# A list scheduler gets a shared SBUF interface and re-measured instruction times

## The chip, the cores and the metric

The kernel runs on one core of a Trainium2 chip. A core has engines that run side by side and wait for each other by semaphores: TensorE (PE in the profile; its weight loads are the row PEld), VectorE (DVE), ScalarE (ACT), GpSimd (POOL) and SyncE (SP), which here issues all DMAs. The metric is the device time in microseconds of one execution. Before the change it is 1359.93 us, the median of three runs (1359.56 to 1360.98).

## The reference, cut to what matters

Two layers of a diffusion block over 256 latent tokens `x` and 256 context tokens `ctx`, 1024 features each, all float32:

```python
for l in range(DEPTH):                                   # 2 layers
    mod_x = silu(c) @ w_ada[l] + b_ada[l]                # shift, scale, gate; the same for ctx
    hx = rms_norm(x, norm_w[l]) * (1 + scale_x) + shift_x
    px = split(hx @ w_in[l], ...)                        # one wide input projection
    y_a = window_sink_attention(...)                     # 8 heads, 2 key heads
    y_b = neighborhood_attention(...)                    # 8 heads, a learned 2-D bias
    y_c = dense_block_attention(...)                     # 8 heads, 2 key heads
    y_d = differential_attention(...)                    # 4 heads of two softmaxes
    branches = [y * silu(gate) for each mixer]
    x = x + gate_x * (sum_n sigmoid(g_n) * (branch_n @ w_br[l, n])) @ w_out[l]
    # the context tokens go the same way, but for the last layer's output
```

Queries and keys of every head are RMS-normed; those of A, C and D get a rotary embedding.

## The kernel before

The program multiplies in float32 by splitting each operand in two float32r parts. A weight chunk of 128 x 1024 comes by DMA as `raw`; its high part `wh` is a rounding copy (ACT or DVE), its low part `wl` is the subtraction `raw - wh` (DVE or POOL). Each matmul of the definition is then three: high by high, high by low, low by high (`mm3`). The chunks are handled in halves of up to 512 columns, and there are 520 of these low-part subtractions. Activations are split in the same way (`hT`, `yT`, `K`, `Q`, `t4k`, `V`). The adaLN products are dot products on DVE (`raw`, `t2k` with `scb`), some on POOL and PE.

All work is written as a sequence of calls, which a `Recorder` collects instead of issuing (class `Recorder`, its engines all record in one line, L270, so in the profile every instruction stands under L270). `alt` makes one operation of each call: the engines that could do it (`ways`), a time for each (`cost`), the operations that it depends on. `copy`, `tt` and `scale` are calls that leave a choice: ACT or DVE for copies (`AV`), DVE or POOL for two-input elementwise work between SBUF tiles (`VG`).

`schedule` is then a list scheduler with a clock of its own. For each engine it looks through the first 60 operations that are available, in order of priority, and takes the first one that could start at once, or else the one that could start first (`ready`: its producers' ends plus a latency from `LAT`, its tiles' slots, its PSUM banks). Where an operation has two ways, it goes to the engine where its end plus `BIAS` (0.55 us for DVE, 0.35 for ACT, 0 for POOL) is earlier. The engine whose candidate can start first gets the next place. `deadlines` works out from the finished schedule how late each operation might start without making TensorE late, and these become the priorities of the next of six tries (`search`); the try whose model ends first is issued, engine by engine, in its order. So the two tables that the change touches, `cost` and the conditions in `ready`, set which engine does what and in which order; the instructions themselves, their shapes and the amount of TensorE's work are the same for every schedule.

On the chip each engine then runs its list in order and waits for semaphores; the planned times are not enforced. GpSimd's `pow` operations (tile `st` with `expo`) are the inverse roots of the norms.

Names in the rows: `ppj`, `psc`, `ptr` are PSUM tiles of projections, scores and transposes; `qk` holds queries or keys before their transposition, `st` columns of statistics, `P` the softmax numerators, `t4k` the transposed numerators, `merged` the gated sum of branches, `bias` mixer B's table.

Of the kernel before, what the change touches and what calls it, by code (L numbers as in the profile page):

```python
# [14 lines left out]
F32R = mybir.dt.float32r  # L15
BF16 = mybir.dt.bfloat16
AF = mybir.ActivationFunctionType
ALU = mybir.AluOpType
# [18 lines left out]
# the grid's tokens go column by column, so that 128 of them are half of the grid. Mixer B's keys: one half, the  # L37
# context, the other half; a half's windows reach 8 columns into the other one
# [5 lines left out]
# token-major groups: blocks of 128 columns (mixer, q/k/v/g, index);  # L44
# "S?" is a mixer's gate path and "G??" a merge gate, both feature-major.
# [34 lines left out]
# the adaLN units computed after a group: the next layer's scale and shift, this layer's gate  # L80
# [9 lines left out]
# ---- instruction order: the program is recorded first, then each engine's order is chosen by list  # L90
# scheduling against a model of the engines, and issued in that order ----
ADA = "DPDDGDDGPGGDDGDD"                       # layer 0, shift and scale: units on VectorE (D), GpSimd (G), TensorE (P)
# [8 lines left out]
GATE = 4096 / 1200.0                         # TensorE runs at half its clock after such a time with little work  # L101
# from the end of an instruction to the start of one that needs it; for TensorE with some margin, so that what it
# has in hand covers a late operand
# [10 lines left out]
def _extent(ap):  # L114
    """(partition range, range of elements within a partition's row) that an access pattern touches"""
# [19 lines left out]
def _run(ap):  # L135
    """elements of the contiguous pieces"""
    return ap.ap[-1][1] if ap.ap[-1][0] == 1 else 1
# [13 lines left out]
# PSUM banks are shared by the three uses, each of which is sure of some  # L151
# [22 lines left out]
class Recorder:  # L174
    def __init__(self, nc, pools, plan=None):
# [3 lines left out]
        if plan is not None:                     # tiles are allocated in the order in which the plan uses them  # L179
            self.made = {}  # L180
            for k, slot in plan.slots:
                self.made[k] = self.make(plan.spec[k], slot)
# [3 lines left out]
        self.acc = {}                            # tile name -> [(op, write, extent)]  # L186
        self.tag = {}                            # tile name -> (tag, bufs)
# [1568 lines left out]
```

## Time and profile before

| | before |
|---|---|
| median of three runs | 1359.93 us |
| profiled execution, first to last instruction (span) | 1355.9 us |
| PE busy | 1266.3 us, 7286 matmuls |
| PEld busy | 1086.5 us |
| DVE busy | 1094.4 us, 2108 instructions |
| ACT busy | 741.8 us, 1738 instructions |
| POOL busy | 696.1 us, 694 instructions |
| mean granted TensorE clock | 0.981 of full speed |
| DMA engines busy | 37.3% |

The time of the profiled execution itself is not listed beside its span; against the median of the runs the span leaves 1359.93 - 1355.9 = 4.0 us for what lies ahead of the first and behind the last instruction. Busy time counts an instruction from its start to its end, so an instruction that is held up after its start counts as busy for as long as it is held. A PE that is busy is not PE at its peak, since matmuls overlap; idle time of an engine counts against the run only where another engine that sets the end waits for it. Stages can be told apart by time: up to about 200 us the adaLN products and the first projection, then the rest of layer 0, from about 800 us layer 1.

### The profile page before, as it was taken

What the parts mean: (1) busy time and instruction counts of PE and PEld (TensorE: products, weight loads), DVE (VectorE), ACT (ScalarE), POOL (GpSimd) and SP (SyncE); (2) the same over time, 40 slices, a digit from 0 to 9 for tenths busy, and PEclk for the clock granted to TensorE, in tenths of its full rate; (3) what the DMA queues carried; (4) which work ended last, traced back from release to release, by engine and by line L of the source; (5) the groups of instructions that cost most, each with busy time, mean ns of one, the idle gap of its engine ahead of it and who ended that gap; (6) DMA issues with size and microseconds to landing.
All of it is one profiled execution on the core that took longest, in us unless ns stands there. A gap on an engine that the chain in (4) does not pass through costs nothing. (4 is left out here: it accounts for less than half of the span.)

```text
span 1355.9 us, 21375 instructions
## 1 busy us (share of the span) xinstructions
PE 1266.3 (93%) x7286; PEld 1086.5 (80%) x7286; DVE 1094.4 (81%) x2108; ACT 741.8 (55%) x1738; POOL 696.1 (51%) x694
## 2 busy tenths in 40 slices
PE   7688999999999999999999999899999899899998
PEld 5466778789877989778777887888889899788897
DVE  7999974974998688995788568798995878886877
ACT  6466843463765346633456345577664556554563
POOL 4784224424554655534364236665754756475643
PEclk8899999999999999999999999999999999999999
DMA  6531133313322432243322266231436534343454
GB/s 244 179 123 42 47 105 98 124 58 114 90 87 94 147 114 72 88 153 100 105 63 78 85 208 203 81 125 51 138 114 176 166 121 140 100 127 105 143 168 172
DMA packets 64576, 160.90 MB, mean 119 GB/s; under 512 B 13482, under 2 KB 24914, under 8 KB 64468
## 3 DMA queue, kind: packets, MB, share of 16 engines
q1 hardware_dynamic: 64468, 159.55, 37.3%
q8 instruction: 57, 0.93, 0.3%
q14 instruction: 51, 0.42, 0.1%
HBM read 157.42 MB, written 5.88 MB: 120 GB/s over the span
## 5 line engine op out<-in xcount | busy, mean ns | idle before, releaser
L270 POOL TENSOR_TENSOR wl<-raw,wh 128x512 fp32r<-128x512 f32 (+2 forms) x233 | 307.6, 1324 | 341.0 <-PE ppj L270 179.6
L270 PE MATMUL ppj<-wh,hT 128*128 128x512 f32 (+2 forms) x1424 | 388.2, 351 | 18.5 <-DVE hT L270 14.2
L270 ACT ACTIVATE wh<-raw 128x512 fp32r<-128x512 f32 (+2 forms) x394 | 233.3, 600 | 250.7 <-PE ppj L270 187.9
L270 PE MATMUL ppj<-hT,wh 128*128 128x512 f32 (+1 forms) x1408 | 368.5, 345 | 0.0
L270 PEld LDWEIGHTS ppj<-wh,hT 128*128 128x128 f32 x1424 | 253.5, 192 | 45.1 <-DVE hT L270 16.8
L270 PEld LDWEIGHTS ppj<-hT,wh 128*128 128x128 f32 x1408 | 244.0, 191 | 27.4 <-ACT t2k L270 0.2
L270 DVE TENSOR_TENSOR wl<-raw,wh 128x512 fp32r<-128x512 f32 (+2 forms) x247 | 199.5, 817 | 77.9 <-PE ppj L270 63.3
L270 PE MATMUL ppj<-wl,hT 128*128 128x512 f32 (+2 forms) x712 | 248.3, 349 | 1.2 <-DVE wl L270 0.7
L270 PE MATMUL ppj<-hT,wl 128*128 128x512 f32 (+1 forms) x704 | 242.9, 345 | 1.8 <-DVE wl L270 1.8
L270 PEld LDWEIGHTS ppj<-wl,hT 128*128 128x128 f32 x712 | 136.8, 192 | 14.8 <-POOL wl L270 1.6
L270 ACT ACTIVATE P<-psc,st 128x512 f32<-128x512 f32 (+2 forms) x192 | 114.8, 601 | 60.8 <-DVE st L270 53.3
L270 PEld LDWEIGHTS ppj<-hT,wl 128*128 128x128 f32 x704 | 134.4, 191 | 16.0 <-DVE wl L270 2.5
L270 PE MATMUL ppj<-yT,wh 128*128 128x512 f32 (+1 forms) x512 | 131.7, 341 | 0.4 <-DVE yT L270 0.4
L270 PE MATMUL psc<-K,Q 128*128 128x512 f32 (+2 forms) x384 | 99.1, 367 | 13.8 <-DVE Q L270 8.4
L270 PE MATMUL ptr<-ident,P 128*128 128x128 f32 x560 | 88.1, 277 | 17.4 <-DVE P L270 12.5
L270 DVE TENSOR_REDUCE st<-psc 128x1 f32<-128x512 f32 (+2 forms) x160 | 102.3, 660 | 1.0
L270 POOL TENSOR_TENSOR st<-st,expo 128x8 f32<-128x8 f32 (+3 forms) x68 | 97.5, 1437 | 2.5
L270 PEld LDWEIGHTS ppj<-yT,wh 128*128 128x128 f32 x512 | 87.5, 189 | 10.6 <-DVE yT L270 0.8
L270 PEld LDWEIGHTS ptr<-ident,P 128*128 128x128 f32 x560 | 64.9, 141 | 37.6 <-DVE P L270 10.3
L270 PEld LDWEIGHTS psc<-K,Q 128*128 128x128 f32 x384 | 63.6, 192 | 33.2 <-DVE Q L270 12.0
L270 PE MATMUL ptr<-t4k,V 128*128 128x256 f32 x480 | 78.4, 289 | 11.1 <-DVE t4k L270 9.0
L270 PE MATMUL ppj<-yT,wl 128*128 128x512 f32 (+1 forms) x256 | 86.8, 339 | 1.0 <-DVE wl L270 1.0
(176 smaller groups left out, 2139.2 us busy)
## 6 DMA issues: line engine op xcount, KB each, us to landing
raw<-in_w_G SPq DMA_DIRECT2D x64, 512.0 KB
raw<-in_w_ada SPq DMA_DIRECT2D x43, 512.0 KB
raw<-in_w_br SPq DMA_DIRECT2D x32, 512.0 KB
raw<-in_w_in_D SPq DMA_DIRECT2D x32, 512.0 KB
raw<-in_w_S SPq DMA_DIRECT2D x24, 512.0 KB
raw<-in_w_in_B SPq DMA_DIRECT2D x32, 384.0 KB
raw<-in_w_out SPq DMA_DIRECT2D x24, 512.0 KB
raw<-in_w_in_A SPq DMA_DIRECT2D x8, 512.0 KB
```

Of the source, the lines that this page charges most:

```text
L270: getattr(getattr(self.nc, eng), fn)(*args, **kw)
```

## The change

Two things change in the planner, nothing in what is computed. `alt` keeps for each way of an operation whether it uses an SBUF interface that DVE and POOL are taken to share (`shares`), and `schedule` lets such an operation start only after the last such operation of the other engine has ended. And `cost` gets other times: float32r matmuls 0.4475 ns a column (before, 1/2400 us, and at least the stationary operand's columns over 1200), ACT 0.08 us more on 64 partitions, DVE 0.06 us more on 64 partitions with PSUM, POOL elementwise 0.1 + 2.35 ns an element (before, 0.15 + 2.1 ns), POOL's `pow` 0.33 + 0.175 us a column, its short `tensor_scalar` 0.23 us. The rest of the diff takes comments out, by which line L270 becomes L271.

```diff
@@ alt
-        op.ways, op.costs = ways, {}
+        op.ways, op.costs, op.port = ways, {}, {}
...
             op.costs[eng] = self.cost(eng, fn, outs, ins, args, kw)
+            op.port[eng] = self.shares(eng, fn, outs, ins, kw)
@@ cost
+        half = outs[0].shape[0] == 64
         if eng == "tensor":
             n = _count(outs[0])
-            f = 1.0 if ins[0].dtype in (F32R, BF16) else (2.0 if fn == "transpose" else 4.0)
-            return max(f * n / 2400.0, _count(ins[0]) / 1200.0) + 0.003
+            if ins[0].dtype in (F32R, BF16):
+                return 0.0028 + n * 0.4475e-3
+            return 0.109 if fn == "transpose" else n * 1.8e-3
         if eng == "scalar":
...
-            return (0.051 if psum else 0.094) + n / 1200.0 + 0.093 * aps
+            return (0.051 if psum else 0.094) + n / 1200.0 + 0.093 * aps + 0.08 * half
...
-            return (62 + n) / 960.0 + (0.06 * aps if fn in ("scalar_tensor_tensor", "tensor_scalar") else 0.0)
+            return (62 + n) / 960.0 + (0.06 * aps if fn in ("scalar_tensor_tensor", "tensor_scalar") else 0.0) + (
+                0.06 * (half and psum))
         if eng == "gpsimd":
             if kw.get("op") == ALU.pow:
-                return 0.3 + 0.165 * n
-            return 0.15 + n * (0.0021 if fn != "tensor_scalar" else 0.0034)
+                return 0.33 + 0.175 * n
+            if fn == "memset":
+                return 0.14
+            if fn == "tensor_scalar":
+                return 0.23 if n < 50 else 0.15 + 0.0103 * n
+            return 0.1 + n * 0.00235
+
+    @staticmethod
+    def shares(eng, fn, outs, ins, kw):
+        if fn == "dma_start" or eng not in ("vector", "gpsimd"):
+            return False
+        if eng == "gpsimd":
+            return kw.get("op") != ALU.pow and _count(outs[0]) >= 16
+        if any(z.space == PSUM for z in outs + ins):
+            return False
+        return fn in ("tensor_copy", "tensor_scalar", "memset") or sum(_count(z) > 1 for z in ins) > 1
@@ schedule
+        port = dict.fromkeys(ENGS, 0.0)
+
         def ready(o, e, s):
             r = max(o.at[e], s)
+            if o.port[e]:
+                r = max(r, port["gpsimd" if e == "vector" else "vector"])
...
             o.fin = t_free[e] = t + c
+            if o.port[e]:
+                port[e] = o.fin
```

What the planner makes of it: of the 520 low-part subtractions 95 go from POOL to DVE and 52 from DVE to POOL; 65 rounding copies `wh` go from DVE to ACT and 27 from ACT to DVE; 62 products that norm or scale `qk` go from DVE to POOL and 20 the other way. Counted by shape, `wl` of 512 columns stands 168 times on POOL before and 106 times after (216 and 278 on DVE); POOL's `wl` of 384 and 256 columns go from 41 to 54 and from 24 to 30; `wh` of 512 columns goes from 74 to 40 on DVE and from 310 to 344 on ACT; POOL's `qk` products with `st` or `gain` go from 35 to 52 (256 columns with `st`), 18 to 28 (128 with `st`) and 5 to 17 (128 with `gain`).

The first place is in layer 1, where mixer D's keys and queries are normed (`qk<-qk,st`) while weight chunks are split. VectorE's list there before:

```order
L270 TENSOR_TENSOR t2k<-of,gT 128x256
L270 TENSOR_TENSOR qk<-qk,st 128x256
L270 TENSOR_TENSOR wl<-raw,wh 128x512
L270 TENSOR_TENSOR yT<-t2k,yT 128x256
L270 TENSOR_TENSOR qk<-qk,st 128x128 x2
L270 CAST wh<-raw 128x512
L270 TENSOR_TENSOR wl<-raw,wh 128x512
```

VectorE's list at the same place now:

```order
L271 TENSOR_REDUCE st<-t2k 128x2
L271 TENSOR_TENSOR wl<-raw,wh 128x512 x4
L271 TENSOR_TENSOR of<-ptr,t2k 64x256
L271 TENSOR_TENSOR V_3083<-ppj,V_3083 128x2x64
L271 TENSOR_TENSOR wl<-raw,wh 128x512 x2
L271 TENSOR_TENSOR Q_3136<-ptr,Q_3136 64x256 x2
L271 CAST yT<-t2k 128x256
```

GpSimd's list at that place before:

```order
L270 TENSOR_TENSOR st<-st,expo 128x8
L270 TENSOR_SCALAR st<-st 128x4
L270 TENSOR_TENSOR qk<-qk,st 128x256
L270 TENSOR_TENSOR st<-st,expo 128x4
L270 TENSOR_TENSOR wl<-raw,wh 128x512
L270 TENSOR_TENSOR bias<-bias,maskB 128x320 x2
L270 TENSOR_TENSOR wl<-raw,wh 128x512 x2
```

GpSimd's list at that place now:

```order
L271 TENSOR_SCALAR st<-st 128x4
L271 TENSOR_TENSOR st<-st,expo 128x4
L271 TENSOR_TENSOR qk<-qk,st 128x128
L271 TENSOR_TENSOR wl<-raw,wh 128x512
L271 TENSOR_TENSOR qk<-qk,gain 128x128
L271 TENSOR_TENSOR bias<-bias,maskB 128x320
L271 TENSOR_TENSOR qk<-qk,st 128x128
L271 TENSOR_TENSOR bias<-bias,maskB 128x320
L271 TENSOR_TENSOR t2k<-of,gT 128x256
L271 TENSOR_TENSOR yT<-t2k,yT 128x256
```

The products `qk<-qk,st` and the split `yT` went from VectorE to GpSimd, and the low parts of 512 columns from GpSimd to VectorE, which now has six of them there.

The second place is in layer 0, where keys and queries of one unit come out of the transposition (64x512, from PSUM) while the first branch is merged. VectorE's list before:

```order
L270 TENSOR_TENSOR wl<-raw,wh 128x512
L270 SCALAR_TENSOR_TENSOR merged<-th,ppj 128x512
L270 CAST K_680<-ptr 64x512
L270 TENSOR_TENSOR K_680<-ptr,K_680 64x512
L270 TENSOR_TENSOR Q_681<-ptr,Q_681 64x512 x2
L270 SCALAR_TENSOR_TENSOR merged<-th,ppj 128x512
L270 TENSOR_TENSOR K_680<-ptr,K_680 64x512 x3
```

VectorE's list there now:

```order
L271 SCALAR_TENSOR_TENSOR merged<-th,ppj 128x512
L271 TENSOR_TENSOR wl<-raw,wh 128x512
L271 TENSOR_TENSOR Q_680<-ptr,Q_680 64x512 x2
L271 SCALAR_TENSOR_TENSOR merged<-th,ppj 128x512
L271 CAST wh<-raw 128x512
L271 TENSOR_TENSOR K_681<-ptr,K_681 64x512 x4
```

The two operations on `Q` now stand ahead of all four on `K`, and the rounding copy of `K` is no longer among them (the buffer numbers differ between the two programs; the tiles are the same).

## Rows read from the trace of the kernel before

**Rows 1.** The page's span, and busy time by engine (share, instructions).

```profile
span 1355.9 us, 21375 instructions
...
PE 1266.3 (93%) x7286; PEld 1086.5 (80%) x7286; DVE 1094.4 (81%) x2108; ACT 741.8 (55%) x1738; POOL 696.1 (51%) x694
```

**Rows 2.** Busy time by stretch: PE, PEld, DVE, ACT, POOL; granted clock, DMA share, GB/s.

```profile
0.00:200.00 200.00, 167.88 (x841) 130.27 (x842) 180.61 (x351) 119.97 (x279) 100.51 (x89) 0.93 0.38 123
200.00:800.00 600.00, 580.89 (x2958) 484.33 (x2957) 460.87 (x848) 303.62 (x709) 269.38 (x259) 1.00 0.32 99
800.00:1300.00 500.00, 465.89 (x3125) 423.74 (x3124) 414.01 (x849) 295.41 (x706) 309.10 (x330) 0.98 0.43 134
1300.00:1356.00 56.00, 51.67 (x368) 48.13 (x366) 38.91 (x61) 22.82 (x45) 17.12 (x17) 1.00 0.51 169
```

**Rows 3.** Waits of PE after 200 us: waiter, releaser, us in total, times, longest.

```profile
PE ptr L270 <- DVE P L270: 10.0, 15, 1.8
PE psc L270 <- DVE Q L270: 8.4, 8, 3.3
PE ptr L270 <- DVE t4k L270: 7.8, 12, 1.3
...
PE ppj L270 <- DVE yT L270: 0.4, 1, 0.4
```

**Rows 4.** The chain that ended last, its longest piece: start, us, engine, matmuls.

```profile
757.41 54.11 PE ppj L270 x234
```

**Rows 5.** Timeline from 1164 to 1168 us, lines of POOL, DVE and PE.

```profile
1164.41 1.18 POOL L270 TENSOR_TENSOR st<-st,expo 128x4 f32<-128x4 f32 x1
...
1164.65 0.41 DVE L270 TENSOR_TENSOR qk<-qk,st 128x256 f32<-128x256 f32 x1
...
1165.56 1.56 POOL L270 TENSOR_TENSOR wl<-raw,wh 128x512 fp32r<-128x512 f32 x1
...
1165.92 2.22 DVE L270 TENSOR_TENSOR qk<-qk,st 128x128 f32<-128x128 f32 x2
...
1167.08 0.91 POOL L270 TENSOR_TENSOR bias<-bias,maskB 128x320 f32<-128x320 f32 x1
...
1167.32 0.33 PE L270 MATMUL ptr<-ident,qk 128*128 128x128 f32 x1 [2.25 <-DVE qk L270]
```

**Rows 6.** DVE's groups by shape: count, busy us, mean ns, idle before.

```profile
L270 DVE TENSOR_TENSOR wl<-raw,wh 128x512 fp32r<-128x512 f32 x216 | 176.5, 827 | 70.7 <-PE ppj L270 60.4 <-ACT wh L270 4.9 <-POOL st L270 1.4
...
L270 DVE TENSOR_TENSOR t4k<-ptr,t4k 128x512 fp32r<-128x512 f32 x112 | 76.1, 680 | 6.3 <-ACT t4k L270 5.6
...
L270 DVE CAST wh<-raw 128x512 fp32r<-128x512 f32 x74 | 54.7, 740 | 7.9 <-PE ppj L270 5.5 <-issue 2.4
...
L270 DVE TENSOR_TENSOR st<-st,nsink 128x1 f32<-128x1 f32 x32 | 9.9, 311 | 0.1
```

**Rows 7.** Timeline, one rounding copy on DVE that nothing holds up.

```profile
348.70 0.43 DVE L270 CAST wh<-raw 128x512 fp32r<-128x512 f32 x1
```

**Rows 8.** Groups by shape on DVE, POOL and ACT, as in group 6.

```profile
L270 POOL TENSOR_TENSOR wl<-raw,wh 128x512 fp32r<-128x512 f32 x168 | 242.8, 1448 | 275.0 <-PE ppj L270 128.5 <-ACT wh L270 44.8 <-issue 19.6
...
L270 ACT ACTIVATE wh<-raw 128x512 fp32r<-128x512 f32 x310 | 193.5, 631 | 184.2 <-PE ppj L270 133.1 <-issue 11.9 <-DVE t2k L270 9.6
...
L270 POOL TENSOR_TENSOR st<-st,expo 128x8 f32<-128x8 f32 x36 | 65.4, 1817 | 1.2
...
L270 DVE RECIPROCAL st<-st 128x1 f32<-128x1 f32 x96 | 14.4, 152 | 0.3
```

**Rows 9.** Timeline from 253.8 to 257 us, lines of DVE and PE.

```profile
253.84 0.67 DVE L270 CAST K<-ptr 64x512 fp32r<-64x512 f32 x1
254.54 0.68 DVE L270 TENSOR_TENSOR K<-ptr,K 64x512 fp32r<-64x512 f32 x1
255.26 1.41 DVE L270 TENSOR_TENSOR Q<-ptr,Q 64x512 fp32r<-64x512 f32 x2
...
256.00 0.85 PE L270 MATMUL psc<-K,Q 128*128 128x512 f32 x3 [3.33 <-DVE Q L270]
```

## The prediction

> **What bounds the kernel now.** I read the busy times first. PE is busy for 1266.3 of 1355.9 us, DVE for 1094.4, and no other engine passes 55% [rows 1]. PE's work is the same for every schedule, so a schedule can only give back what PE loses: 1355.9 - 1266.3 = 89.6 us of idle time, and what it runs at the lower clock. By stretch [rows 2], PE is idle for 200 - 167.9 = 32.1 us up to 200 us, 19.1 us up to 800, 34.1 us up to 1300 and 4.3 us at the end (the last evictions and the store). Behind 800 us the mean clock is 0.98: over 500 us that is 10 us at full speed lost to stretches at 1.2 instead of 2.4 GHz.
>
> Who is waited for? Of PE's waits after 200 us [rows 3] twelve lines name DVE; from 10.0 us for `P` down to 0.4 us for `yT` they sum to 43.8 us. The eight others name POOL and ACT and are short. So DVE is what PE waits for, though DVE has idle time of its own, 1355.9 - 1094.4 = 261.5 us. The question is why it is late.
>
> The timeline at one of the longest waits shows it [rows 5]. At 1165.56 POOL starts a low part of 512 columns. DVE comes to two products `qk<-qk,st` of 128 columns at 1165.92 and needs 2.22 us for the two, although one of 256 columns took 0.41 us a moment before. The first cannot end before POOL's subtraction does, at 1167.12, and the second not before POOL's next instruction, which began at 1167.08 and ends at 1167.99. PE stands for 2.25 us. DVE and POOL hold each other out for whole instructions.
>
> How much of this is in DVE's busy time is read by comparing equal sizes [rows 6]: `t4k`, with 512 columns and one operand in PSUM, takes 680 ns on average; `wl`, with 512 columns and both in SBUF, 827. That is 216 x 0.147 = 31.8 us of being held. A rounding copy `wh` alone takes 0.43 us [rows 7], on average 0.740 [rows 6]: 74 x 0.31 = 22.9 us. These two groups hold 55 us of waiting; they are not all.
>
> **The change part by part.** *Load.* By the counts of the section on the change POOL loses 62 low parts of 512 columns at 1.448 us [rows 8], 89.8 us, and gets 13 of 384 and 6 of 256 columns (by columns, estimates of 1.09 and 0.72 us: 14.1 and 4.3 us), and 39 `qk` products, which I put at 0.72 us for 17 of 256 columns and 0.36 for 22 of 128, by the same price a column: 20.2 us. Net, POOL has 51 us less of 696. DVE gets 62 x 0.68 = 42.2 us by `t4k` [rows 6] and gives 34 x 0.43 = 14.6 us of copies to ACT [rows 7], 19 smaller low parts (13 x 0.51 + 6 x 0.34 = 8.7 us) and the 39 products (17 x 0.41 + 22 x 0.28, estimates from the 0.41 us of [rows 5], about 13 us): net +6 us without waits. ACT gets 34 x 0.631 = 21.5 us [rows 8] on 742, which its idle time hides: it is busy for 55%. None of these loads lies on the path by itself; what counts is when DVE is late.
>
> *Order with the interface known.* It has no row in the trace of before, so I bound it. From above: every wait for DVE after 200 us goes, and with it the lower clock: 43.8 + 10 = 54 us. From below: since only the order is issued and not the planned times, the two engines may meet as by chance as before, just more rarely; POOL holds the interface for 51 of 696 us less, 7%, and 7% of 43.8 is 3 us. Nothing excludes a loss either; it is a rival below. Between these ends I take two places. At the first one [rows 5] the products now stand on POOL itself, and their 2.25 us of being held there can't arise in that form. At the second [rows 9], PE waited 3.33 us for `Q` while DVE did the copy and one subtraction of `K` first, 0.67 and 0.68 us; now `Q` stands ahead of `K`, worth about 1.35 us. Together 3.6 of 5.6 us, 64%. These are two of the longest waits, DVE now has six low parts in a row at the first place, and an order that ends one wait makes others, so I take half rather than 64%: 22 us of waits and 5 us of clock.
>
> *The first 200 us.* Half of PE's idle time there is the start, which the order hardly changes: weights come in one fixed order, and the adaLN products fill DVE (180.6 of 200 us busy [rows 2]). I count nothing.
>
> *The times.* The longest unbroken run of matmuls, all of 512 columns, gives 54.11 / 234 = 0.231 us each [rows 4]. The old table says 0.216, the new one 0.232. So in the old plan PE ran 7% too fast against its helpers, and DVE, by the waits, too fast as well. The correction has no price of its own in the sum; the slower rival is built on it.
>
> **Where a rule of the notes and the rows meet.** The root operations `pow` do not hold DVE up in the trace: while POOL was in one of 1.18 us, DVE's product took its usual 0.41 us [rows 5]. The new rule leaves `pow` out, in keeping with that. The Trainium skill, "SBUF — State Buffer", section "Who interferes with whom", says that a VectorE instruction with two SBUF inputs contends with any GpSimd instruction that reads SBUF, for the whole instruction. By the page the change would leave some 65 us of holding unplanned in the largest `pow` group alone (36 x 1.817 us, [rows 8]) and I would expect less than half; by the row it leaves none, and I go by the row.
>
> On one-column operations the trace says the opposite of the new rule: a two-input `st<-st,nsink` of one column takes 311 ns on average [rows 6], a reciprocal of one column 152 [rows 8]. The new function counts only inputs of more than one element, so these stay unplanned: 32 x 0.16 = 5 us of waiting that the change cannot take away, part of the half that I leave. The same page names two SBUF inputs, whatever their size, and the trace agrees.
>
> **The rivals.** *Chance meetings stay.* The chip does not keep the plan's times: weights and semaphores come earlier or later, and DVE and POOL meet about as often as their load says. For it speaks that nothing enforces the times; against it that both lists changed so that work which would collide now often stands on one engine. The gain is 3 us, up to a third of what I forecast: 1348 to 1357 us; at the low end this is no change at all.
>
> *Nearly all waits go.* DVE is idle for 261 us and has much work on PSUM operands, which is not held up (`t4k`, [rows 6]), so an order with few meetings is possible. Then 54 us: 1306 us. Against it: POOL's and DVE's users together are still a large share of the time, and the one-column ones aren't planned.
>
> *Lost margin, slower.* With matmuls planned 0.015 us too short each, a block of 24 of 512 columns gave every helper 0.36 us that the plan didn't count on. That margin goes with the new table, and helpers are placed as late as their own times allow. Place: the matmuls that need scores' and transposes' operands (`psc`, `ptr`), where PE's waits are now. There are 70 waits in the 20 lines of [rows 3]; each longer by 0.36 us costs 25 us, and less the 3 us of the lower load the run takes 1382 us. It decides where the plan's helper times are short by more than the plan's own latencies leave. Against it: the interface wait, which was the largest error in the helpers' times, is now planned.
>
> **How the numbers follow.** The profiled execution spans 1355.9 us; the median of the runs is 4.0 us more, and I carry these 4 us along. Forecast: 1359.9 - 22 - 5 = 1333 us; with the ends of the half (a third to three quarters of 54 us) 1319 to 1345. Chances: forecast 0.46; chance meetings with a gain that shows 0.18; nearly all waits gone 0.12; no change 0.08; slower 0.16. A measurement of this kernel can tell about 0.2% from no change, here 2.7 us. Faster by more than that is 0.46 + 0.18 + 0.12 = 0.76, within it 0.08, slower 0.16. The range for 8 in 10 leaves out the lower half of the large gain (0.06) and most of the slower case (0.13): 1308 to 1367 us.
>
> **What would show it.** If I am right, DVE's busy time falls by 40 us or more although its work grows by 6: `wl` of 512 columns comes from 827 ns down towards 690, `wh` on DVE from 740 towards 430, one-column `st<-st,nsink` stays near 300. The lines of PE's waits that name DVE sum to about 22 us after 200 us, and the clock behind 800 us is 0.99. If meetings stay by chance, these means stay within 10% of before. If the margin is lost, `wl` gets faster and PE's waits at `ptr` and `psc` grow all the same, in number above all. I am wrong in the large if PE's idle time up to 200 us moves by more than 10 us, or if ACT, with 21 us more, becomes what PE waits for.

## The result and the profile after

The changed kernel takes 1321.45 us, the median of four runs (1319.68 to 1325.38), beside 1360.28 us for the kernel before on the same chip (four runs, 1359.56 to 1360.98). The ratio is 0.9721, with a 95% interval of 0.9705 to 0.9738: 38.8 us less. Forecast were 27 us less (1333) in a range of 1308 to 1367. Sign and mechanism held, the size was 1.4 times the forecast, and behind that size stand three errors that partly cancel; the experiments take them apart.

The page of the kernel after, its span and busy times by engine (share, instructions), to be read beside [rows 1]:

```profile
span 1317.9 us, 21363 instructions
...
PE 1243.6 (94%) x7286; PEld 1083.4 (82%) x7286; DVE 1003.8 (76%) x2074; ACT 757.1 (57%) x1761; POOL 626.9 (48%) x705
```

The span is 38.0 us shorter. PE's idle time fell from 89.6 to 74.3 us, by 15.3. The other 22.7 us came out of PE's *busy* time, 1266.3 to 1243.6, with the same 7286 matmuls. DVE's busy time fell by 90.6 us, although by the counts it has some 6 us more to do: it was being held, and is held less now.

Busy time by stretch in the kernel after (PE, PEld, DVE, ACT, POOL; then granted clock, DMA share, GB/s), against [rows 2]:

```profile
0.00:200.00 200.00, 156.36 (x816) 124.72 (x817) 165.80 (x342) 119.59 (x281) 94.92 (x90) 0.91 0.37 121
200.00:800.00 600.00, 593.43 (x3044) 500.69 (x3043) 441.56 (x879) 312.96 (x721) 230.72 (x247) 1.00 0.35 107
800.00:1270.00 470.00, 450.48 (x3135) 418.45 (x3134) 364.35 (x804) 303.43 (x720) 287.87 (x355) 0.99 0.45 137
1270.00:1318.00 48.00, 43.31 (x296) 39.55 (x294) 32.09 (x50) 21.09 (x40) 13.35 (x13) 1.00 0.51 173
```

Behind 200 us PE is idle for 6.6 + 19.5 + 4.7 = 30.8 us where it was 57.5. In the first 200 us it is idle for 43.6 us where it was 32.1: that part got worse by 11.5 us. The mean clock behind 800 us is 0.99 where it was 0.98; in the first 200 us it is 0.91 where it was 0.93. Over the whole span it is 0.981 in both.

The waits of PE after 200 us in the kernel after (waiter, releaser, us in total, times, longest), against [rows 3]:

```profile
PE ptr L271 <- DVE P L271: 5.1, 5, 3.3
PE ptr L271 <- DVE Q L271: 4.4, 2, 3.5
PE ptr L271 <- DVE t4k L271: 2.8, 4, 0.9
PE ptr L271 <- ACT P L271: 2.6, 2, 1.8
PE psc L271 <- ACT P L271: 2.0, 3, 1.2
PE psc L271 <- DVE Q L271: 1.9, 2, 1.4
```

Together the lines that name DVE hold 17.9 us in 20 waits, where they held 43.8 us in 59.

DVE's and POOL's groups by shape in the kernel after (count, busy us, mean ns of one, idle before), against [rows 6] and [rows 8]:

```profile
L271 DVE TENSOR_TENSOR wl<-raw,wh 128x512 fp32r<-128x512 f32 x278 | 204.5, 748 | 85.8 <-PE ppj L271 58.8 <-ACT wh L271 14.0 <-issue 8.0
...
L271 DVE TENSOR_TENSOR t4k<-ptr,t4k 128x512 fp32r<-128x512 f32 x112 | 76.5, 683 | 5.7 <-ACT t4k L271 4.2
...
L271 DVE CAST wh<-raw 128x512 fp32r<-128x512 f32 x40 | 19.6, 494 | 4.7 <-PE ppj L271 2.5 <-POOL wl L271 2.0
...
L271 DVE TENSOR_TENSOR st<-st,nsink 128x1 f32<-128x1 f32 x32 | 7.1, 225 | 0.1
...
L271 POOL TENSOR_TENSOR wl<-raw,wh 128x512 fp32r<-128x512 f32 x106 | 140.4, 1329 | 227.2 <-PE ppj L271 110.9 <-ACT wh L271 61.4 <-issue 13.7
```

The same instruction on the same data got shorter: a low part on DVE 827 to 748 ns, one on POOL 1448 to 1329, a rounding copy on DVE 740 to 494. `t4k`, which has an operand in PSUM, stayed (680, now 683). So the two engines stand in each other's way less, in both directions.

At the second place, DVE and PE from 254.7 us in the kernel after (start, us, engine; in brackets what ended the idle time before it), against [rows 9]:

```profile
254.75 0.68 DVE L271 TENSOR_TENSOR wl<-raw,wh 128x512 fp32r<-128x512 f32 x1
...
256.24 1.41 DVE L271 TENSOR_TENSOR Q<-ptr,Q 64x512 fp32r<-64x512 f32 x2 [0.81 <-ACT Q L271]
...
257.00 0.39 PE L271 MATMUL ppj<-hT,wl 128*128 128x512 f32 x1
257.23 0.63 PE L271 MATMUL ppj<-hT,wh 128*128 128x512 f32 x2
257.68 0.69 DVE L271 SCALAR_TENSOR_TENSOR merged<-th,ppj 128x512 f32<-128x512 f32 x1
257.69 0.75 PE L271 MATMUL psc<-K,Q 128*128 128x512 f32 x3
```

`Q` ends at 257.65, and PE takes up the scores at 257.69 without a pause, where it had waited 3.33 us. At the first place, which lies at 1135.5 us in this kernel, PE's wait for `qk` is gone: between 1080 and 1180 us PE waits three times, for 1.0 us together.

The PE rows show one thing more. A matmul of 512 columns has a record of 0.39 us, but its successor starts 0.23 us after it (257.00 and 257.23). The ends of these records are modelled; a pause of up to some 0.16 us behind a matmul lies within its record and is counted as busy. How much of the 22.7 us of "busy" time this is can be counted over the matmuls of both traces, by the distance from each start to the next, beyond what is usual for the shape. At the full clock, 526 matmuls before were followed more than 15 ns later than usual, with 52.8 us of that within their records; after, there are 422 with 39.7 us. At a granted clock below 0.9, in whole or in part at the lower level of 1.2 GHz, there were 154 matmuls, with 20.9 us beyond the usual distance; now there are 100, with 13.7 us. So 13.1 of the 22.7 us are delays that the records hide, 7.2 us are matmuls that no longer run at the lower clock, and the rest is spread too thinly to be sorted. The Trainium skill, "Perfetto Trace Analysis", section "Identifying the Most-Contended Engine", says that the share in which matmuls are busy is no good measure of how close TensorE is to its limit, because they are pipelined. The trace agrees, with these 13.1 us.

The start of the kernel after is the place that got worse. First PE's longest line of waits in the first 200 us of before, then that of after:

```profile
PE ppj L270 <- DVE hT L270: 13.5, 6, 8.5
```

```profile
PE ppj L271 <- ACT hT L271: 34.2, 5, 22.5
```

The timeline of after shows what `hT` waits for (ACT, DVE and POOL between 31 and 56 us, and the matmul that waited):

```profile
31.59 3.34 POOL L271 TENSOR_TENSOR t4k<-V,scb 128x1024 f32<-128x1024 f32 x1
...
32.64 2.44 DVE L271 TENSOR_SCALAR mods<-st,bcol 128x2 f32<-128x2 f32 x2
34.99 2.37 DVE L271 TENSOR_SCALAR mods<-st,bcol,nwc 128x2 f32<-128x2 f32 x1
35.00 2.34 POOL L271 TENSOR_TENSOR V<-V,scb 128x1024 f32<-128x1024 f32 x1
...
50.42 3.20 POOL L271 TENSOR_TENSOR V<-V,scb 128x1024 f32<-128x1024 f32 x1
...
51.36 2.29 DVE L271 TENSOR_SCALAR mods<-st,bcol,nwc 128x2 f32<-128x2 f32 x1
53.56 0.21 DVE L271 TENSOR_SCALAR mods<-st,bcol 128x2 f32<-128x2 f32 x1
...
54.01 1.09 ACT L271 ACTIVATE t2k<-merged,mods 128x256 f32<-128x256 f32 x2 [9.24 <-DVE mods L271]
...
55.81 0.79 PE L271 MATMUL ppj<-wh,hT 128*128 128x512 f32 x1 [22.45 <-ACT hT L271]
```

`mods` has two columns and takes 0.21 us when nothing holds it (53.56). During a product of 1024 columns on POOL it takes 2.3 us and more (32.64 for two, 34.99, 51.36), each time until POOL's product ends, and ACT, `hT` and PE stand in the row behind it. But these three rows are 7.1 us of a wait of 22.45 us, and the kernel before has the same holding in its start:

```profile
38.50 2.48 DVE L270 TENSOR_SCALAR mods<-st,bcol,nwc 128x2 f32<-128x2 f32 x2
```

Another part is the order: from 43.6 to 51.4 us DVE works through four adaLN products of 1024 columns before it comes to this `mods`.

### The profile page after: what moved, and what is told of

Read it like the earlier page. It is cut to its first block, busy times and chain, and to the rows that moved or that the text cites. A ratio compares the mean times of both kernels' runs of the same rounds, so it can differ in the third digit from the quotient of the medians.

```text
span 1317.9 us, 21363 instructions
## 1 busy us (share of the span) xinstructions
PE 1243.6 (94%) x7286; PEld 1083.4 (82%) x7286; DVE 1003.8 (76%) x2074; ACT 757.1 (57%) x1761; POOL 626.9 (48%) x705
## 5 line engine op out<-in xcount | busy, mean ns | idle before, releaser
L271 PE MATMUL ppj<-wh,hT 128*128 128x512 f32 (+2 forms) x1424 | 387.4, 350 | 34.6 <-ACT hT L271 34.2
L271 ACT ACTIVATE wh<-raw 128x512 fp32r<-128x512 f32 (+2 forms) x432 | 254.6, 603 | 270.5 <-PE ppj L271 196.7
L271 POOL TENSOR_TENSOR wl<-raw,wh 128x512 fp32r<-128x512 f32 (+2 forms) x190 | 221.1, 1172 | 311.6 <-PE ppj L271 164.3
L271 PE MATMUL ppj<-hT,wh 128*128 128x512 f32 (+1 forms) x1408 | 363.3, 342 | 0.0
L271 PEld LDWEIGHTS ppj<-wh,hT 128*128 128x128 f32 x1424 | 253.0, 191 | 60.2 <-ACT hT L271 35.1
L271 DVE TENSOR_TENSOR wl<-raw,wh 128x512 fp32r<-128x512 f32 (+1 forms) x290 | 210.7, 739 | 86.7 <-PE ppj L271 59.7
L271 PEld LDWEIGHTS ppj<-hT,wh 128*128 128x128 f32 x1408 | 241.4, 189 | 26.8 <-PE ppj L271 0.2
L271 PE MATMUL ppj<-wl,hT 128*128 128x512 f32 (+2 forms) x712 | 247.8, 350 | 1.6 <-POOL wl L271 1.6
L271 PE MATMUL ppj<-hT,wl 128*128 128x512 f32 (+1 forms) x704 | 241.1, 343 | 0.4 <-DVE wl L271 0.3
L271 ACT ACTIVATE P<-psc,st 128x512 f32<-128x512 f32 (+2 forms) x192 | 114.7, 601 | 58.8 <-DVE st L271 53.4
L271 PEld LDWEIGHTS ppj<-wl,hT 128*128 128x128 f32 x712 | 136.1, 192 | 13.9 <-POOL wl L271 2.2
L271 PEld LDWEIGHTS ppj<-hT,wl 128*128 128x128 f32 x704 | 133.0, 189 | 14.7 <-DVE wl L271 0.7
L271 PE MATMUL ppj<-yT,wh 128*128 128x512 f32 (+1 forms) x512 | 130.2, 339 | 0.3 <-ACT yT L271 0.3
L271 DVE TENSOR_REDUCE st<-psc 128x1 f32<-128x512 f32 (+2 forms) x160 | 101.2, 661 | 0.8
L271 PE MATMUL psc<-K,Q 128*128 128x512 f32 (+2 forms) x384 | 95.3, 357 | 5.6 <-ACT P L271 2.0
L271 PE MATMUL ptr<-ident,P 128*128 128x128 f32 x560 | 89.7, 277 | 11.5 <-DVE P L271 6.1
L271 POOL TENSOR_TENSOR st<-st,expo 128x8 f32<-128x8 f32 (+3 forms) x68 | 96.2, 1418 | 3.6
L271 PEld LDWEIGHTS ppj<-yT,wh 128*128 128x128 f32 x512 | 87.1, 188 | 10.8 <-ACT yT L271 0.5
L271 PEld LDWEIGHTS ptr<-ident,P 128*128 128x128 f32 x560 | 67.2, 142 | 27.6 <-ACT P L271 8.4
L271 POOL TENSOR_TENSOR ru<-qk,rtab 128x256 f32<-128x256 f32 (+1 forms) x34 | 25.0, 735 | 134.8 <-ACT qk L271 134.1
L271 PE MATMUL ppj<-yT,wl 128*128 128x512 f32 (+1 forms) x256 | 86.6, 339 | 0.0
L271 DVE TENSOR_REDUCE st<-t2k 128x4 f32<-128x256 f32 (+3 forms) x114 | 42.0, 381 | 53.7 <-ACT t2k L271 51.2
```

Of the source, the lines that this page charges most:

```text
L271: getattr(getattr(self.nc, eng), fn)(*args, **kw)
```

## The experiments

My theory at this point: the gain comes from the interface alone; the plan's order ends most of the holding; the true times bring nothing by themselves. The rivals: the true times do it (the holding was only a sign of an otherwise bad order); any other order would do as well (the kernel before was an unlucky one); and, on the loss side, the "lost margin" of the prediction eats a part of the gain. Each ratio is against runs of the kernel before on the same chip, which had medians of 1359.4, 1360.2 and 1360.5 us in the three sets.

**The interface without the new times** (`port_only`). Against the changed kernel, `cost` is put back to what it was; `shares` and the condition in `ready` stay:

```diff
         if eng == "tensor":
             n = _count(outs[0])
-            if ins[0].dtype in (F32R, BF16):
-                return 0.0028 + n * 0.4475e-3
-            return 0.109 if fn == "transpose" else n * 1.8e-3
+            f = 1.0 if ins[0].dtype in (F32R, BF16) else (2.0 if fn == "transpose" else 4.0)
+            return max(f * n / 2400.0, _count(ins[0]) / 1200.0) + 0.003
...
-            return 0.1 + n * 0.00235
+            return 0.15 + n * (0.0021 if fn != "tensor_scalar" else 0.0034)
```

> The planner knows of the interface, with the old instruction times. If the interface is what counts, most of the 39 us gained is here: 1325 to 1338 us, and the mean of wl of 512 columns on VectorE falls from 827 to below 770 ns. If the corrected times are what counts, little is here: 1350 to 1360 us. If the gain is the luck of one order among many, it can lie anywhere, and the two kernels with shaken times, run beside this one, spread over more than 20 us.

Measured: 1303.53 us (1302.47 to 1303.98), ratio 0.9591, interval 0.9574 to 0.9608. The interface alone gives 55.9 us, 18 more than the whole change and more than I had expected of it: the new times cost something. DVE's line and the first 100 us of this kernel (columns as above):

```profile
L271 DVE TENSOR_TENSOR wl<-raw,wh 128x512 fp32r<-128x512 f32 x270 | 196.2, 741 | 85.6 <-PE ppj L271 59.0 <-issue 15.6 <-ACT wh L271 3.9
```

```profile
0.00:100.00 100.00, 65.05 (x303) 50.62 (x304) 75.91 (x122) 47.96 (x101) 51.74 (x45) 0.83 0.51 170
```

After 200 us PE's waits for DVE are down to 7.0 us in 14 places. The start is as poor as in the kernel after: 303 matmuls begun in 100 us.

**The new times without the interface** (`cost_only`). Against the changed kernel:

```diff
-            if o.port[e]:
+            if False:
                 r = max(r, port["gpsimd" if e == "vector" else "vector"])
```

> The new instruction times without the interface: shares is computed and not used. If the interface is what counts: 1345 to 1360 us, wl of 512 columns on VectorE stays at 800 ns or more. If the times are what counts: 1325 to 1338 us. If the lost margin of the prediction is real, it shows here alone: above 1365 us, with more waits of TensorE at psc and ptr than before.

Measured: 1356.53 us (1353.8 to 1357.36, ten runs), ratio 0.9979, interval 0.9968 to 0.9989. DVE's low parts by shape:

```profile
L271 DVE TENSOR_TENSOR wl<-raw,wh 128x512 fp32r<-128x512 f32 x250 | 194.1, 786 | 72.9 <-PE ppj L271 62.2 <-issue 5.4 <-POOL merged L271 1.6
...
L271 DVE CAST wh<-raw 128x512 fp32r<-128x512 f32 x65 | 44.7, 690 | 9.0 <-PE ppj L271 5.4 <-issue 2.2 <-POOL wl L271 1.3
```

The low part at 786 ns is somewhat shorter than I had expected, but PE's waits for DVE stand at 44.6 us in 51 places, as before the change. True times alone are worth 0.2%, and the lost margin, which was to show in this kernel by a time above 1365 us, does not show here. The page's busy times answer another rival, that POOL's lighter load is what helps:

```profile
PE 1258.8 (93%) x7286; PEld 1082.4 (80%) x7286; DVE 1090.0 (81%) x2142; ACT 735.0 (54%) x1733; POOL 650.2 (48%) x665
```

POOL is as lightly loaded here as in `port_only` (646.7 us), and the gain is 2.9 us instead of 55.9.

**Another order, the same knowledge** (`after_jit`, `before_jit`, `port_jit`). In the changed kernel, in the kernel before and in `port_only`, each planned time is multiplied by a number between 0.99 and 1.01 that depends on the operation's place in the program. Nothing else changes, but the search comes out at another order:

```diff
-            op.costs[eng] = self.cost(eng, fn, outs, ins, args, kw)
+            op.costs[eng] = self.cost(eng, fn, outs, ins, args, kw) * (0.99 + 0.02 * ((op.i * 613 + 977) % 1009) / 1009)
```

> The changed kernel with every planned time multiplied by a number between 0.99 and 1.01 that depends on the operation's place: nothing is known better or worse, only the order comes out another way. If the gain is systematic: within 12 us of the changed kernel, 1310 to 1334 us. If it is the luck of one order: up to 1345 us.

> The kernel before with the same shaking of its planned times. If the gain is systematic: 1348 to 1372 us, far from the shaken changed kernel. If the changed kernel was a lucky order or the one before an unlucky one: below 1340 us.

> The interface with the old times, each multiplied by a number between 0.99 and 1.01. The changed kernel moved by 9 us under the same shaking. If the old times are really better with the interface, this one stays below 1310 us. If the 18 us between port_only and the changed kernel are the luck of one order, it lies anywhere from 1303 to 1325 us.

Measured: `after_jit` 1312.20 us (1311.34 to 1312.32), ratio 0.9654, interval 0.9637 to 0.9672; `before_jit` 1357.36 us (1354.43 to 1361.94, ten runs), 0.9988, 0.9975 to 1.0001; `port_jit` 1305.99 us (1304.58 to 1306.84), 0.9608, 0.9588 to 0.9628. The kernel before was no unlucky draw: its neighbour is 2 us away from it. But one order's luck is worth 2 to 9 us, and the changed kernel is the slower of its two. So a difference below 9 us between two single orders is read below only where a row of the trace shows its place.

**Which of the new times costs the 18 us** (`port_pe`, `port_helpers`). `port_pe` has the interface, PE's new time, and the old times of ACT, DVE and POOL; `port_helpers` has the interface, PE's old time, and the helpers' new ones. The edit of `port_helpers` against the changed kernel is the first part of the diff of `port_only` (`if eng == "tensor":`) alone, that of `port_pe` all the rest of it.

> The interface, old times for the helpers, the new time for TensorE alone. If it is the margin of TensorE's old, too short time that makes port_only faster than the changed kernel, this loses it: 1315 to 1325 us. If the helpers' new times are at fault, it stays at 1300 to 1308 us.

> The interface, the new times for the helpers, the old time for TensorE: the changed kernel with the margin put back. If the margin counts: 1300 to 1308 us, with fewer waits of TensorE than in the changed kernel. If the helpers' new times are at fault: 1315 to 1325 us.

Measured: `port_pe` 1327.59 us (1325.25 to 1330.46), ratio 0.9769, interval 0.9743 to 0.9795; `port_helpers` 1302.65 us (1302.06 to 1303.32), 0.9583, 0.956 to 0.9606. Now there are six kernels that all know the interface:

| PE planned at | kernels, us | mean |
|---|---|---|
| 0.216 us, as before (7% too fast) | `port_only` 1303.5, `port_jit` 1306.0, `port_helpers` 1302.7 | 1304.1 |
| 0.232 us, as measured | the changed kernel 1321.5, `after_jit` 1312.2, `port_pe` 1327.6 | 1320.4 |

The two rows don't overlap; with the interface known, the true PE time costs 16.3 us on the mean, while the helpers' times bring 0.9 us (`port_only` to `port_helpers`). PE's waits after 200 us in `port_pe` (columns as above):

```profile
PE ptr L271 <- ACT P L271: 4.2, 11, 0.7
PE ptr L271 <- DVE t4k L271: 3.4, 7, 0.9
PE psc L271 <- DVE Q L271: 3.2, 5, 2.0
PE psc L271 <- DVE K L271: 2.7, 6, 1.1
```

Many short waits, at the transposes and scores: 32 for DVE with 17.4 us, where `port_only` has 14 with 7.0. That is how the lost margin was to show. It is not all: of the 27.1 us between the two spans 13.9 are in PE's busy time (1241.5, here 1255.4). My reading is that with a PE that is planned too fast, each helper's operand is asked for a little earlier than PE will be there, and what comes late on the chip is covered. The runs fit it but do not show it by itself, and why the same time cost nothing in `cost_only`, without the interface, is open.

**Margin in another form** (`after_lat`) **and more of it** (`late_pe93`). `after_lat` keeps the true times and plans 0.3 us more from the end of an ACT, DVE or POOL instruction to the PE instruction that needs it:

```diff
-    "scalar": (0.42, 0.15, 0.15, 0.18),
-    "vector": (0.41, 0.13, 0.127, 0.16),
-    "gpsimd": (0.36, 0.075, 0.06, 0.1),
+    "scalar": (0.72, 0.15, 0.15, 0.18),
+    "vector": (0.71, 0.13, 0.127, 0.16),
+    "gpsimd": (0.66, 0.075, 0.06, 0.1),
```

> The changed kernel, with 0.3 us more planned latency from ScalarE, VectorE and GpSimd to TensorE: a margin put into the hand-over and not into the matmuls' time, about what a block of 24 matmuls gains by the old table. If port_only and port_helpers are faster because operands are asked for earlier, this one comes down from 1321 to 1300 to 1311 us. If the matmuls' planned speed counts in another way, it stays at 1315 to 1327 us.

Measured: 1308.14 us (1305.87 to 1309.03), ratio 0.9621, interval 0.9602 to 0.9639: 13.3 us less than the changed kernel, which fits the margin. Since `after_jit` is only 4.1 us above it, the part that is beyond one order's luck is not settled by this run.

`late_pe93` is `port_late` (next) with PE's old planned time times 0.93, so another 7% too fast:

```diff
-            return max(f * n / 2400.0, _count(ins[0]) / 1200.0) + 0.003
+            return 0.93 * (max(f * n / 2400.0, _count(ins[0]) / 1200.0) + 0.003)
```

> port_late with TensorE's planned time 7% shorter still, that is twice the margin that the old table had against the trace. If the margin works by making the planner ask for operands earlier, there may be more to have: 1283 to 1292 us and fewer waits of TensorE. If the old table's 7% was enough, 1291 to 1299 us. If too much margin spoils the choice between engines, above 1299 us.

Measured: 1298.15 us (1296.66 to 1298.99), ratio 0.9548, interval 0.9531 to 0.9565, 3.7 us above `port_late`: within one order's luck. One margin of 7% is worth 16 us. What a second one is worth is not settled: this kernel loses 7.4 us in its first 100 us (rows further down) and wins about half of that back behind them.

**The start** (`port_late`). `port_only` with the interface left out of the plan for the first 100 us:

```diff
-            if o.port[e]:
+            if o.port[e] and max(r, t_free[e]) > 100.0:
                 r = max(r, port["gpsimd" if e == "vector" else "vector"])
```

> The interface with the old times, but ignored by the planner for what it starts before 100 us. In all three kernels so far that know the interface, TensorE stands for 22 to 25 us in one piece within the first 60 us, and is busy for 61 to 65 of the first 100 us against 76 before. If the interface in the plan makes the start worse, the first 100 us come back to 72 us or more of TensorE and the time is 1290 to 1298 us. If the pause has another cause (the order of weights, the sums on GpSimd), the time stays at 1300 to 1308 us with the pause in it.

Measured: 1294.42 us (1293.66 to 1294.86), ratio 0.9523, interval 0.9505 to 0.9542, the fastest of all and 9.1 us below `port_only`. The first 100 us of this kernel, then of the kernel before:

```profile
0.00:100.00 100.00, 72.69 (x318) 54.03 (x318) 87.35 (x137) 49.70 (x105) 66.05 (x61) 0.81 0.51 177
```

```profile
0.00:100.00 100.00, 75.66 (x340) 55.67 (x341) 90.09 (x142) 54.95 (x116) 66.98 (x62) 0.86 0.54 183
```

PE's wait for `hT` in this kernel's first 200 us:

```profile
PE ppj L271 <- ACT hT L271: 15.2, 4, 8.2
```

It was 28.7 us in `port_only` and 34.2 in the changed kernel; with the line that names DVE's `hT` (6.7 us here, 1.3 in `port_only`) it is 21.9 against 30.0. Here the gain has its place: in the first 100 us PE is busy for 72.7 us where it was 65.1 in `port_only`, and 7.6 us of the 9.1 are found there. In this pair of orders, planning the interface costs about 9 us at the start. Two more of the kernels leave it out of the first 100 us, and they do not agree with each other (`late_pe93`, then `late_onecol`):

```profile
0.00:100.00 100.00, 65.27 (x312) 50.84 (x313) 87.64 (x137) 47.19 (x101) 64.25 (x57) 0.81 0.52 177
0.00:100.00 100.00, 77.96 (x339) 58.27 (x340) 89.84 (x142) 54.98 (x116) 70.06 (x61) 0.83 0.54 183
```

The first has a start as poor as `port_only`, with 30.1 us of waits for `hT`; the second starts better than the kernel before. Over all runs, PE is busy for 61.4 to 66.4 us of the first 100 in the seven kernels that plan the interface from the start, for 65.3, 72.7 and 78.0 in the three that leave it out there, and for 71.3 to 78.0 in the four that do not plan it at all. So the direction is borne out on the whole, and the 9 us are the size in one pair of orders. My reading is that DVE and POOL both work through adaLN products there without a break, and that taking turns makes both late; which of their operations lost most by it was not tried.

**The one-column operations** (`late_onecol`). `port_late` with every two-input operation counted, whatever its size:

```diff
-        return fn in ("tensor_copy", "tensor_scalar", "memset") or sum(_count(z) > 1 for z in ins) > 1
+        return fn in ("tensor_copy", "tensor_scalar", "memset") or len(ins) > 1
```

> port_late, and two-input operations of VectorE on one column count as users of the interface too. They still take about 270 ns on average where an undisturbed one takes 150, 64 of them: some 8 us of holding that is not planned. If planning them helps, their means fall below 220 ns and the time is 1286 to 1292 us; if they are too short to matter, 1291 to 1299 us.

Measured: 1312.14 us (1308.21 to 1313.76), ratio 0.9648, interval 0.9625 to 0.9671: 17.7 us slower than `port_late`. The operation that I had named did get shorter, in this kernel:

```profile
L271 DVE TENSOR_TENSOR st<-st 128x1 f32<-128x1 f32 x32 | 8.6, 279 | 1.5 <-ACT P L271 1.4
L271 DVE TENSOR_TENSOR st<-st,nsink 128x1 f32<-128x1 f32 x32 | 6.8, 225 | 0.1
```

`st<-st,nsink` went from 332 ns in `port_late` to 225, but its neighbour `st<-st` of one column from 222 to 279, and PE's longest wait after 200 us in this kernel is one of 6.6 us for DVE's `Q`. Behind its first 100 us, where it is 5.3 us ahead of `port_late`, this kernel loses about 23 us: PE's waits after 200 us are 26.2 us where they were 12.5, and PE's busy time is 8.1 us longer. The one-column operations are held up as I had read (in the kernel before, `st<-st,nsink` took 144 ns while POOL was idle and 457 ns otherwise), and planning them as holders of the interface did not pay here. Whether that is the rule or one order's luck (17.7 us would be the largest seen) stays open.

**Does the interface do it on the chip, in the old order?** (`pool_writes`). This is the run that leaves planning out. The order is that of the kernel before, instruction by instruction; only POOL's 233 low-part subtractions are replaced, each by three fills of the same tile with zeros. These low parts are left out of the result's computation. What changes is that POOL, at about the same places and for somewhat longer in total, writes SBUF there and reads nothing:

```diff
+REPEAT = 3
...
+        if eng == "gpsimd" and fn == "tensor_sub" and args[1].tensor.name.startswith("raw"):
+            for _ in range(REPEAT):
+                self.nc.gpsimd.memset(args[0].bitcast(F32), 0.0)
+            return
```

> The order of the kernel before, instruction for instruction; but GpSimd's 233 low parts wl are not computed: each is three writes of zeros to the same tile, so that GpSimd is kept busy there without reading SBUF (these low parts are left out of the products). If GpSimd's instructions hold VectorE out by the interface they both read through, VectorE's wl of 512 columns falls from 827 to below 760 ns, TensorE's waits for VectorE behind 200 us fall below 30 us, and the time is 1320 to 1342 us with no change of order at all. If what VectorE waits for is something else than GpSimd's reading, its mean stays above 800 ns and the time within 8 us of 1360.

Measured: 1302.67 us (1302.48 to 1304.38), ratio 0.9586, interval 0.9566 to 0.9606: 57.8 us less with the old order and the old plan, more than I had expected of it. The page's busy times, then the groups by shape in this kernel:

```profile
PE 1247.9 (96%) x7286; PEld 1077.2 (83%) x7286; DVE 1005.6 (77%) x2108; ACT 739.0 (57%) x1738; POOL 731.5 (56%) x1160
```

```profile
L275 DVE TENSOR_TENSOR wl<-raw,wh 128x512 fp32r<-128x512 f32 x216 | 168.7, 788 | 86.5 <-PE ppj L275 75.0 <-issue 5.1 <-ACT wh L275 1.8
...
L275 DVE CAST wh<-raw 128x512 fp32r<-128x512 f32 x74 | 46.0, 623 | 8.3 <-PE ppj L275 8.2
```

POOL is busier than before by 35 us, DVE less by 89. PE's waits for DVE after 200 us are 15.9 us in 30 places. The low part's mean is 788 ns, above the 760 that I had set as the limit; the records behind it tell why. Of DVE's `wl`, the 41 that began during a row of these fills took 683 ns on average, 81 that began while nothing of POOL's ran took 690; 51 that began during one of POOL's remaining elementwise products (`pow` apart) took 1115. For a `wl`, a POOL that only writes is not there; the rest of the mean comes from the products that were left. A rounding copy is another matter: 40 copies `wh` that began during a row of fills took 643 ns, 17 that began with POOL idle 419. One of each, in the timeline of this kernel:

```profile
331.93 3.61 POOL L273 MEMSET wl<- 128x512 f32 x6 [1.04 <-PE ppj L275]
...
333.17 0.73 DVE L275 CAST wh<-raw 128x512 fp32r<-128x512 f32 x1
...
334.03 0.69 DVE L275 TENSOR_TENSOR wl<-raw,wh 128x512 fp32r<-128x512 f32 x1
```

Within one row of fills the copy takes 0.73 us, where [rows 7] has 0.43, and the subtraction its usual 0.69. The Trainium skill, "SBUF — State Buffer", section "Who interferes with whom", says that a two-input operation of VectorE contends with GpSimd instructions that read SBUF and not with those that only write, while a copy or cast can enter a mode that uses both ports and can then contend with GpSimd. These rows agree with both halves.

Two other things change with the fills. They read neither `raw` nor `wh` and need not wait for `wh`; but in the kernel before PE waited for a low part of POOL's only once after 200 us, for 0.4 us. And the mean granted clock is 0.990 where it was 0.981: by the two spans that is some 13 us (an estimate), and no run tells whether it follows from PE's shorter waits or from the zeros in the products. Some 45 us are left without it. So the theory stands without any plan: what DVE lost in the kernel before, it lost in the main to POOL's reads.

## Why the prediction was right, and where its steps were off

**What bounds the kernel** was right. DVE was late because POOL held it. `pool_writes` takes the holding away in the old order and gains 57.8 us; the interface in the plan gains 55.9.

**The order with the interface known** was right as a mechanism and too small as a term. Of PE's 43.8 us of waits for DVE I took half, 22 us; 25.9 went in the changed kernel, and the clock behind 800 us came back as forecast (0.98 to 0.99), though what it gave there was lost again in the first 200 us (0.93 to 0.91). But the upper bound, 43.8 + 10 = 54 us, was no bound: `port_only` gains 55.9 us and `port_late` 65.8. The step that failed is in the prediction's first part: that a schedule "can only give back what PE loses" was right, but I took the idle time of the records, with the lower clock, for all that PE loses. PE's busy time fell by 22.7 us in the changed kernel and by 23.3 us (1266.3 to 1243.0) in `port_late`. By the count above, 13.1 and 17.4 us of that are delays that lie within the records of the matmuls ahead of them, and 7.2 and 3.0 us matmuls at the lower clock. [Rows 4] had the number that should have warned me: 0.231 us from start to start, to be held against the length of a matmul's record, 0.39 us in the rows of the second place above.

**The first 200 us** were counted at nothing; PE's idle time there grew by 11.5 us, more than the 10 us that I had named as being wrong in the large. I had argued that the order hardly changes the start since weights and adaLN products fill it. The products do fill DVE, and the order did change the start: leaving the interface out of it gave 9.1 us back in `port_late`, though not in `late_pe93`.

**The times** had no price in the sum and were made the slower rival, at 25 us. The loss is there and has about the size: with the interface known, the true PE time costs 16.3 us on the mean of three orders each, 24.1 from `port_only` to `port_pe`, 18.8 from `port_helpers` to the changed kernel. Without the interface it does not show (`cost_only`). What was wrong with the rival is what it was set against, the 3 us of a lighter load; against 55.9 us it can't turn the sign. Its point of decision was wrong as well: it costs 18.8 us even where the helpers' times are the new ones.

Put together, the changed kernel is 55.9 us of interface (which contains the 9 us lost at the start), 0.9 us of helper times and -18.8 us of margin. These are the steps of one path through single orders (`port_only`, `port_helpers`, the changed kernel), so they add up to 38.0 us by themselves, and each holds the luck of its order. My 27 us came from a term that was half its size and a loss that I left out of the sum; that it came near is in part luck, since the two cancel. Two small sums were off as well, and nothing else hangs on them: a third of 54 us is 18, so the upper end of the half is 1342 us and not 1345, and a gain of a third of the forecast ends at 1351 us and not 1348.

**The rivals.** That meetings stay by chance falls: PE's waits for DVE more than halved, and the copy went from 740 to 494 ns. Something of it is true: `wl` of 512 columns stayed at 748 ns, within 10% of 827, where `t4k` has 683, so meetings are rarer and not gone. That nearly all waits go is what `port_only` shows, at 1303.5 us for the 1306 that I had given it; with the new PE time it did not come.

**What would show it.** DVE busy by 40 us or more less: 90.6. `wl` towards 690: 748. `wh` towards 430: 494. Waits for DVE about 22 us: 17.9. ACT as what PE waits for: after 200 us no, over the whole run yes by name, since the longest line of waits is now the 34.2 us for ACT's `hT` at the start; ACT itself waited for DVE's `mods` there. One-column `st<-st,nsink` near 300: 225, missed; in `port_late` it is 332 with the same rule, so its mean goes with the order, not with the rule.

**The root operations.** I went by the row, and it held: a `pow` on POOL doesn't hold DVE. Over the whole trace of before, 37 `wl` of 512 columns began during a `pow` and took 681 ns on average, and 107 that began while POOL was idle took 686; [rows 5] was no exception. The Trainium skill, "SBUF — State Buffer", section "Who interferes with whom", has any GpSimd instruction that reads SBUF hold a two-input one; for `pow` the trace says otherwise. No run planned `pow` as a holder, so what that would have cost was not tried.

## What to carry to other kernels

Compare the mean of one instruction form with that of a like form that has an operand in PSUM; if it is longer, VectorE and GpSimd hold each other, and an order that has them take turns gave back more here than all of PE's visible waits for VectorE. Before taking idle time as the most that can be won, hold an engine's busy time against its count times the distance from start to start, shape by shape. And a planner's wrong number can be its margin: put the true time in and add the margin elsewhere, or measure the two separately.

## What the runs showed of the hardware that I had not expected

- A GpSimd instruction that only writes SBUF (a fill) leaves VectorE's two-input subtraction alone (683 ns during it, 690 without), but makes a rounding copy longer (643 ns against 419).
- Holding doesn't go by size: a `tensor_scalar` of two columns, 0.21 us by itself, took 2.29 us during a GpSimd product of 1024 columns.
- With the same 7286 matmuls, PE's busy time went from 1266.3 to 1241.5 us (`port_only`): of that, 11.5 us were delays that don't show as idle time, and 11.3 us matmuls at the lower clock.
- An order that is planned with all times off by at most 1% ran 2 to 9 us from its neighbour.
